# A two-layer decoder trunk in float32: a second seven-product slice in the feed-forward blocks, with its products set between plain ones

## The chip, the cores and the metric

The kernel runs on one core of one Trainium2 chip. The metric is the device time of one execution in microseconds (us); lower is better. TensorE (PE in the profile) multiplies, VectorE (DVE), ScalarE (ACT) and GpSimd (POOL) prepare its operands, SyncE (SP) issues most transfers from HBM.

## The reference

Two decoder layers on 256 tokens of width 2048, all in float32. `wide` below stands for 5632.

```
for l in range(2):
    h = rms_norm(x, attn_norm[l])
    za, zq, zk, zv, zc = split(h @ w_in[l])      # 2048 x 5632: gated mixer, attention, conv
    ya = gelu(za) -> u, v;  u * (tril(ws) @ layer_norm(v) + bs)      # 4 groups of 128
    yb = softmax(q0 k0) v - lam * softmax(q1 k1) v, with rotary q, k # 4 heads
    yc = bg * conv3(cg * hc)
    x = x + (group_rms(ya, yb, yc) * mix_norm[l]) @ w_out[l]         # 2048 x 2048
    h = rms_norm(x, ffn_norm[l])
    x = x + (silu(h @ w_gate[l]) * (h @ w_up[l])) @ w_down[l]        # 2048 x wide, wide x 2048
return rms_norm(x, final_norm)
```

## The kernel before

**Tiling.** Every weight matrix is cut into blocks of 512 x 512 (`CW = 512`): four weight tiles of 128 rows by 512 columns, 1 MB in float32, laid out so that a block is contiguous. The 256 tokens are two halves of 128 (`NT = 2`). TensorE holds a 128 x 128 piece of the activations and streams 512 weight columns through it.

**Splitting.** The matmuls take operands of type float32r. Each float32 operand is split into a high part of that type and the rest, the low part, and a product is three matmuls: high by high, low by high, high by low (`products`, L220 to L222). Weights are split on the fly, half a block (two weight tiles, 128 x 1024) at a time; this is a *job*: ScalarE writes the high part `wh` (L169), VectorE subtracts it for the low part `wl` (L170). A plain job feeds 2 token halves x 2 weight tiles x 3 = 12 matmuls. The pool `wsp` holds five split halves, and `ahead(4)` emits the split of the job four ahead before the matmuls of the present one: a split can begin when the job five before it has left its buffer.

**Seven products.** In each feed-forward block `f` (512 of the 5632 hidden columns, eleven blocks a layer) the gate and up weights of one of the four slices `k` of 512 input rows (`SEVEN = 1`, the second) are multiplied by Strassen's scheme. It takes the 2 x 2 blocks (two token halves by two halves of the slice's rows; gate and up as the columns) with seven products in place of eight. Each of the seven has one job of its own and 6 matmuls (`seven_products`). The sums of activation blocks (`block_sums`) are made once a layer; the sums of weight halves are made for each block: three by VectorE (L164), and one by a transfer that adds in flight (`accum_op=ALU.add`, on POOL's queue, L175). Four products go to the tiles `p` and are combined on VectorE (L828 to L831), three go straight into the accumulators `c`.

**Order.** Each engine works its own queue in order; a scheduler places the instructions of the program in these queues near to program order. Side work (norms, transposes, attention) is put into a list by `later`, and `step` runs one entry after each job. `need` runs the list as far as an operand requires. The input projection's column chunks are worked in the order of `IN_ORDER`: two value chunks, then query and key chunks of attention, chunk 1 (the gated mixer's `v`: gelu, layer norm), 9, 10 and 8 (conv), 0 (the gated mixer's `u`). What follows a chunk, such as the layer norm of chunk 1 (L724 to L753), is emitted when its matmuls are done.

**Loads.** One transfer of 1 MB per block on SP's queue (512 KB and 256 KB at the start), four buffers of 1 MB (`wfp`). After each feed-forward block the 16 pieces of its transposed result are moved by SP's queue as well (`moved_transposed`).

Of the kernel before, what the change touches and what calls it, by code (L numbers as in the profile page):

```python
# [18 lines left out]
P = 128  # L19
# [34 lines left out]
def trunk_kernel(ctx: ExitStack, tc, x, positions, w_in, gmlp_ln_g, gmlp_ln_b,  # L54
# [11 lines left out]
    wfp = ctx.enter_context(tc.tile_pool(name="wf", bufs=4))  # L66
    wsp = ctx.enter_context(tc.tile_pool(name="wsplit", bufs=5))
    bpool = ctx.enter_context(tc.tile_pool(name="blk", bufs=27))
# [11 lines left out]
    IN_ORDER = [6, 7, 2, 4, 3, 5, 1, 9, 10, 8, 0]  # L80
# [8 lines left out]
    SEVEN = 1  # L89
    wsrc = []  # L90
    onto = {}
    jobs = []

    def wblock(w, k, c):
        return w[c, k].rearrange("p (k c) -> p k c", k=4)

    def plain(src):
        jobs.extend((len(wsrc), h, None) for h in range(2))
        wsrc.append(src)

    def seven(src1, src2):

        i, j = len(wsrc), len(wsrc) + 1
        onto[len(jobs)] = (i, j)
        jobs.extend([(i, 0, None), (j, 0, (j, 1)), (j, 1, None), (i, 1, None), (i, 0, None),
                     (j, 1, (i, 0)), (i, 1, (j, 1))])
        wsrc.extend([src1, src2])

    for l in range(L):
        for n, k in PAIR if l else FIRST:
            plain(wblock(w_in[l], k, IN_ORDER[n]))
        for c in IN_ORDER[2:]:
            for k in range(NX):
                plain(wblock(w_in[l], k, c))
        for n, k in PAIR:
            plain(wblock(w_out[l], MIX_ORDER[k], n))
        for c in range(2, NX):
            for k in MIX_ORDER:  # L120
                plain(wblock(w_out[l], k, c))
        for hv in PARTS:
            for f in hv:
                for k in range(NX):
                    if k == SEVEN:
                        seven(wblock(w_gate[l], k, f), wblock(w_up[l], k, f))
                    else:
                        plain(wblock(w_gate[l], k, f))
                        plain(wblock(w_up[l], k, f))
            for c, k in pair(len(hv)):  # L130
                plain(wblock(w_down[l], hv[k], c))
            for c in range(2, NX):
                for f in hv:
                    plain(wblock(w_down[l], f, c))

    wfull, whalf, lows = {}, {}, {}
    state = {"load": 0, "split": 0, "use": 0}

    def load_weights(n):
        while state["load"] < min(n, len(wsrc)):  # L140
            i = state["load"]
            wf = wfp.tile([P, 4, CW], F32, tag="wf", name=f"wf{i}")
            w = 2 if i < 4 else 4
            for k in range(0, 4, w):
                nc.sync.dma_start(out=wf[:, k:k + w], in_=wsrc[i][:, k:k + w])
            wfull[i] = wf
            state["load"] += 1

    def load_weight_part(i, k0, k1, queue=nc.sync):
        if i not in wfull:  # L150
            wfull[i] = wfp.tile([P, 4, CW], F32, tag="wf", name=f"wf{i}")
            state["load"] = max(state["load"], i + 1)
        queue.dma_start(out=wfull[i][:, k0:k1], in_=wsrc[i][:, k0:k1])

    def split_weights(n):
        while state["split"] < min(n, len(jobs)):
            j = state["split"]
            i, h, more = jobs[j]
            load_weights(max(i, more[0] if more else 0) + 1)
            wf = wfull[i][:, 2 * h:2 * h + 2]  # L160
            if more is not None:
                i2, h2 = more
                with tc.issue_after(lows[j - 2].ins):
                    nc.vector.tensor_tensor(wf, wf, wfull[i2][:, 2 * h2:2 * h2 + 2], op=ALU.add)  # L164
# [8 lines left out]
            lows[j] = state["dve"]  # L173
            if j in onto:
                nc.gpsimd.dma_start(out=wf, in_=wsrc[onto[j][1]][:, 0:2], accum_op=ALU.add)  # L175
            state["split"] += 1

    def ahead(n):

        j = min(state["use"] + n, len(jobs) - 1)  # L180
        split_weights(j + 1)
        load_weights(jobs[state["use"]][0] + 4)
# [53 lines left out]
    def seven_products(dst, operand, sums):  # L236

        sh, sl = sums
        S = [[[x[:, n, k] for k in range(2)] for x in (sh, sl)] for n in range(4)]
        lhs = [block(operand, 0, 0), S[2], S[3], block(operand, 1, 0), S[0], S[1], block(operand, 1, 1)]  # L240
        for (acc, first, last), x in zip(dst, lhs):
            ahead(4)
            products(acc, *x, state["use"], first, last)
            whalf.pop(state["use"])
            state["use"] += 1
            step()
# [32 lines left out]
    load_weight_part(0, 0, 1, nc.scalar)  # L279
# [24 lines left out]
    for c in range(NX):  # L304
        xt = blk([P, 4, S], f"xt{c}")
        th, tl = blk([P, 4, S], f"tha0_{c}", F32R), blk([P, 4, S], f"tla0_{c}", F32R)
        for k in range(0, 4, 2):
            nc.sync.dma_start(out=xt[:, k:k + 2], in_=x_t[c, :, k:k + 2])
            if c == 0:
                if k == 0:  # L310
                    nc.sync.dma_start(out=gT, in_=gains)
                load_weight_part(0, 1 + k, 2 + k)
                if k == 0:
                    load_weight_part(0, 2, 3)
# [15 lines left out]
        load_weights(min(c + 1, 3))  # L330
# [6 lines left out]
    def rstd(dst, src, scale, eps, n):  # L337

        nc.gpsimd.tensor_scalar(dst, src, scale, eps, op0=ALU.mult, op1=ALU.add)
        nc.gpsimd.tensor_tensor(dst, dst, neghalf[:, :n], op=ALU.pow)  # L340

    def rotary_tables(pos_i, frq):
# [34 lines left out]
        turns(ang, 1.0)  # L377
        for j in range(4):
            axpy(ang, n, -cs[j], ang)
        V.tensor_tensor(ang, ang, rem, op=ALU.add)  # L380
        turns(ang, 1.0)
        for j in range(4):
            axpy(ang, n, -cs[j], ang)
        lim = 3.1415925
        V.tensor_scalar(ang, ang, lim, -lim, op0=ALU.min, op1=ALU.max)
# [9 lines left out]
        return waves  # L395
# [79 lines left out]
    def moved_transposed(src, dst, key, gap):  # L475
# [28 lines left out]
    def block_sums(stat, key, gcol):  # L504
# [16 lines left out]
        def split():  # L521
            nc.scalar.copy(sh, sr)
            nc.vector.tensor_tensor(sl, sr, sh.bitcast(F32), op=ALU.subtract)
            stat["sums"] = (sh, sl)
# [32 lines left out]
    def norm_chunk(c, ssq, gcol, stat, tag, sums=False):  # L557
# [3 lines left out]
        if sums:  # L561
            block_sums(stat, (tag, "sums"), gcol + 4 * c)(o)
# [26 lines left out]
    waves = rotary_tables(*tabs)  # L589

    for l in range(L):
# [21 lines left out]
        later(token_scales, ("r", l))  # L613
        lng, lnb, cw, wT = layer_loads(l)
        if l == 0:
            later(lambda: lambdas(load_lambda()))
        later(rotary_scales, ("rt", l), wait=17 if l == 0 else 0)
# [179 lines left out]
        def projected(c, acc):  # L797
            add_residual(acc, c)
            norm_chunk(c, ssq, 32 + 16 * l, stat, f"f{l}", c == SEVEN)

# [7 lines left out]
        for hi, hv in enumerate(PARTS):  # L808
            mids = {}
            for f in hv:  # L810
                P1, P5, P7, P6 = (trp.tile([P, CW], F32, tag="tr", name=f"p{n}_{f}") for n in (1, 5, 7, 6))
                C = [[accp.tile([P, CW], F32, tag="acc", name=f"c{f}_{n}{t}") for t in range(NT)] for n in range(2)]
                for k in range(SEVEN):
                    need(fkeys[k])
                    for n in range(2):
                        weight_tile(C[n], stat[fkeys[k]], [k == 0] * NT, False)
                need(fkeys[SEVEN])
                need((f"f{l}", "sums"))
                alone = (True, True)
                seven_products([(P1, *alone), (P7, *alone), (C[1][0], False, False), (C[0][0], False, False),  # L820
                                (P5, *alone), (P6, *alone), (C[0][1], False, False)],
                               stat[fkeys[SEVEN]], stat["sums"])
                if rf is None:
                    rf = token_rstd(ssq, "rf")
                sg, mid = blk([P, NT, CW], "sg"), blk([P, NT, CW], "mid")

                nc.scalar.copy(sg[:, 0], P1)
                nc.vector.tensor_tensor(mid[:, 0], sg[:, 0], P6, op=ALU.add)  # L828
                nc.vector.tensor_tensor(sg[:, 1], mid[:, 0], P7, op=ALU.add)
                nc.vector.tensor_tensor(mid[:, 0], P5, mid[:, 0], op=ALU.subtract)  # L830
                nc.vector.tensor_tensor(mid[:, 1], P5, sg[:, 1], op=ALU.subtract)  # L831
                rest = range(SEVEN + 1, NX)
                for k in rest:
                    need(fkeys[k])
                    for n in range(2):
                        weight_tile(C[n], stat[fkeys[k]], [False] * NT, k == rest[-1])
                        for t in range(NT if k == rest[-1] else 0):
                            if n == 0:
                                nc.vector.tensor_tensor(sg[:, t], sg[:, t], C[0][t], op=ALU.add)
                                nc.scalar.activation(sg[:, t], sg[:, t], AF.Silu, scale=rf[:, t:t + 1])  # L840
                            else:
                                nc.vector.tensor_tensor(mid[:, t], mid[:, t], C[1][t], op=ALU.add)
                for t in range(NT):
# [97 lines left out]
```

## Time and profile before

| | |
|---|---|
| median of 3 runs | 2123.53 us (2121.87 to 2125.17) |
| the profiled execution | 2121.89 us, of which the span from the first to the last instruction is 2119.8 us |
| TensorE | busy 2098.0 us, 99% of the span, 9264 matmuls |
| VectorE / ScalarE / GpSimd | 74% / 54% / 9% |
| mean granted TensorE clock | 0.997 of full speed |
| transfers | 440.54 MB, mean 208 GB/s |

The busy times of engines overlap, so they don't add up to the span. A matmul's busy time includes the end of its pipeline, which the next one covers; its true cost is the distance between the starts of two. A VectorE instruction likewise is listed a little longer than its slot when the next one follows at once.

### The profile page before, as it was taken

Reading aid. Unit: us, or ns where it says so; the run is one execution under the profiler, and the core shown is the slowest. Engines: PE = TensorE matmul, PEld = TensorE weight load, DVE = VectorE, ACT = ScalarE, POOL = GpSimd, SP = SyncE. Lnnn points to the kernel's source line nnn. Section 1 sums busy time; section 2 is a strip of 40 time slices with the busy share of each in tenths; the row PEclk is TensorE's granted clock in tenths of the full one; section 3 lists DMA queues with packets and bytes.
Section 4 is the critical chain, followed back from the end, with each engine's and each line's share of the span. In section 5 each row is a group of like instructions: output and inputs, shape, how many; then the busy total and the mean of one; then the engine's idle time right before and its main releaser. Section 6 shows DMA issues by size and latency. Waiting matters only on the chain.

```text
span 2119.8 us, 25036 instructions
## 1 busy us (share of the span) xinstructions
PE 2098.0 (99%) x9264; PEld 1735.2 (82%) x9264; DVE 1559.2 (74%) x1926; ACT 1137.6 (54%) x1479; POOL 201.0 (9%) x199
## 2 busy tenths in 40 slices
PE   8999999999999999999999999999999999999998
PEld 7887888888888888888888878888888888888886
DVE  5787778877567775678767878788775678756874
ACT  6556468555444543454755664675554454534453
POOL 6123410000000000000001234000000000000002
PEclk9999999999999999999999999999999999999999
DMA  8654555676556656566565445556655566655663
GB/s 317 240 177 161 179 211 176 219 250 218 199 180 245 220 203 221 205 222 204 204 235 190 160 158 197 201 186 247 219 200 220 207 220 215 227 204 208 212 231 123
DMA packets 83013, 440.54 MB, mean 208 GB/s; under 512 B 13518, under 2 KB 25294, under 8 KB 34252
## 3 DMA queue, kind: packets, MB, share of 16 engines
q1 hardware_dynamic: 79580, 427.16, 55.3%
q0 software_dynamic: 3168, 11.54, 3.2%
q8 instruction: 72, 1.18, 0.2%
q14 instruction: 49, 0.40, 0.1%
q10 hardware_dynamic: 144, 0.26, 0.0%
HBM read 423.19 MB, written 2.10 MB: 201 GB/s over the span
## 4 chain that ended last, share of the span: by engine, by line
PE 86%; POOL 2%; DVE 2%; ACT 1%; issue 1%; DMA 0%; SPq 0%; POOLq 0%; ACTq 0%
PE acc L221 14%; PE acc L220 14%; PE acc L222 14%; PE c L221 13%; PE c L220 13%; PE c L222 13%; PE p L221 2%; PE p L220 2%; PE p L222 2%; DVE wl L170 1%; PE op L679 0%; ACT wh L169 0%; DMA x<-xh 0%; ACT bom L456 0%; POOL gsq L573 0%
## 5 line engine op out<-in xcount | busy, mean ns | idle before, releaser
L170 DVE TENSOR_TENSOR wl<-wf,wh 128x1024 fp32r<-128x1024 f32 (+1 forms) x836 | 1029.5, 1245 | 455.7 <-ACT wh L169 451.6
L169 ACT CAST wh<-wf 128x1024 fp32r<-128x1024 f32 (+1 forms) x836 | 868.4, 1050 | 837.4 <-PE acc L222 397.9
L220 PE MATMUL c<-wh,thf 128*128 128x512 f32 x1144 | 445.0, 389 | 0.0
L221 PE MATMUL c<-wl,thf 128*128 128x512 f32 x1144 | 445.0, 389 | 0.0
L222 PE MATMUL c<-wh,tlf 128*128 128x512 f32 x1144 | 445.0, 389 | 0.0
L220 PE MATMUL acc<-wh,tha 128*128 128x512 f32 x704 | 280.6, 399 | 1.4 <-ACT wh L169 1.4
L221 PE MATMUL acc<-wl,tha 128*128 128x512 f32 x704 | 275.4, 391 | 2.9 <-DVE wl L170 2.9
L222 PE MATMUL acc<-wh,tla 128*128 128x512 f32 x704 | 275.3, 391 | 0.0
L220 PE MATMUL acc<-wh,thd 128*128 128x512 f32 x704 | 273.9, 389 | 0.0
L221 PE MATMUL acc<-wl,thd 128*128 128x512 f32 x704 | 273.9, 389 | 0.0
L222 PE MATMUL acc<-wh,tld 128*128 128x512 f32 x704 | 273.9, 389 | 0.0
L220 PEld LDWEIGHTS c<-wh,thf 128*128 128x128 f32 x1144 | 214.7, 188 | 44.6
L222 PEld LDWEIGHTS c<-wh,tlf 128*128 128x128 f32 x1144 | 214.8, 188 | 44.5
L221 PEld LDWEIGHTS c<-wl,thf 128*128 128x128 f32 x1144 | 214.8, 188 | 44.5
L221 PEld LDWEIGHTS acc<-wl,tha 128*128 128x128 f32 x704 | 133.0, 189 | 31.1 <-DVE wl L170 4.2
L220 PEld LDWEIGHTS acc<-wh,tha 128*128 128x128 f32 x704 | 132.7, 189 | 29.2 <-ACT wh L169 1.9
L222 PEld LDWEIGHTS acc<-wh,tla 128*128 128x128 f32 x704 | 132.7, 188 | 28.4
L220 PEld LDWEIGHTS acc<-wh,thd 128*128 128x128 f32 x704 | 132.2, 188 | 27.4
L222 PEld LDWEIGHTS acc<-wh,tld 128*128 128x128 f32 x704 | 132.2, 188 | 27.4
L221 PEld LDWEIGHTS acc<-wl,thd 128*128 128x128 f32 x704 | 132.2, 188 | 27.4
L175 POOL DMA_DIRECT2D wf<-in_w_up_dram x22 | 19.4, 880 | 1324.3 <-DVE wl L170 1324.3
L221 PE MATMUL acc<-wl,thm 128*128 128x512 f32 x256 | 99.7, 390 | 0.1
(193 smaller groups left out, 1867.9 us busy)
## 6 DMA issues: line engine op xcount, KB each, us to landing
wf<-in_w_gate_dram SPq DMA_DIRECT2D x88, 1024.0 KB, 4.8
wf<-in_w_up_dram SPq DMA_DIRECT2D x88, 1024.0 KB, 6.3
wf<-in_w_down_dram SPq DMA_DIRECT2D x88, 1024.0 KB, 4.9
wf<-in_w_in_dram SPq DMA_DIRECT2D x84, 1024.0 KB, 4.8
wf<-in_w_out_dram SPq DMA_DIRECT2D x32, 1024.0 KB, 4.7
wf<-in_w_up_dram POOLq DMA_DIRECT2D x22, 512.0 KB, 5.7
bod<-btd SPq DMA_DIRECT2D x352, 32.0 KB, 1.9
wf<-in_w_in_dram SPq DMA_DIRECT2D x6, 512.0 KB, 8.1
```

The costliest lines, as they stand in the source:

```text
L169: state["act"] = nc.scalar.copy(wh[:, k:k + w], wf[:, k:k + w])
L170: state["dve"] = nc.vector.tensor_tensor(wl[:, k:k + w], wf[:, k:k + w], wh[:, k:k + w].bitcast(F32), op=ALU.subtract)
L175: nc.gpsimd.dma_start(out=wf, in_=wsrc[onto[j][1]][:, 0:2], accum_op=ALU.add)
L220: nc.tensor.matmul(acc, xh[k], wh[:, k, :], start=first and k == 0, stop=False)
L221: nc.tensor.matmul(acc, xh[k], wl[:, k, :], start=False, stop=False)
L222: nc.tensor.matmul(acc, xl[k], wh[:, k, :], start=False, stop=last and k == 1)
```

## The change

- `SEVEN` becomes a list: block 0 of a layer keeps slice 1 alone, blocks 1 to 10 use the scheme for slices 0 and 1. Both slices add into the same four tiles `p`, which are combined once.
- The jobs of a block are written out by `ffn_order`: of the eight last plain jobs, the first seven are each followed by one product of each seven-product slice (order 1, 7, 5, 6, 3, 2, 4). Products are taken job by job (`half_products`).
- For slice 0 the sum for product 7 is made by a second transfer that adds in flight (`plus`); product 6 and product 4 have their sums from VectorE, as in slice 1, where product 7 has it too.
- Weights are loaded half a block (512 KB) at a time into tiles of the common pool `blk` (35 in place of 27 tiles of 4 KB a partition, `wfp` is gone), by a window of 20 half-job units and at most 10 tiles.
- Half of the 16 moves after a block go to POOL's queue.
- `IN_ORDER`: the gated mixer's chunk 1 and conv's chunk 9 change places.
- At the start, the second half of the rotary table's arithmetic (`near`) goes behind the first token scale on POOL.
- At the end, the last norm's sum over the first three chunks is taken ahead.

```diff
-    IN_ORDER = [6, 7, 2, 4, 3, 5, 1, 9, 10, 8, 0]
+    IN_ORDER = [6, 7, 2, 4, 3, 5, 9, 1, 10, 8, 0]
...
-    SEVEN = 1
+    WINDOW = 20
+    ROOM = 10
+    SEVEN = [[1], [0, 1]]
+    P1, P7, P5, P6, P3, P2, P4 = range(7)
+    def ffn_order():
...
+            own = [("plain", f, k, n, h) for k in range(NX) if k not in sv for n in range(2) for h in range(2)]
+            for j, it in enumerate(own):
+                items.append(it)
+                if 0 <= j - len(own) + 8 < 7:
+                    items.extend(("seven", f, j - len(own) + 8, k) for k in sv)
...
+        if p == P1:
+            onto[len(jobs)] = whalf_of(w_up[l], k, f, 0)
+            job(half(0, 0), size=1)
...
+        elif p == P7:
+            if k == 0:
+                i = half(1, 0)
+                plus[i] = whalf_of(w_up[l], k, f, 1)
+                first[i] = len(jobs) - 6
+                job(i, size=1)
+            else:
+                job(half(1, 0), half(1, 1), size=1)
...
+    def load_weights(upto, room=None):
+        while state["load"] < len(loads) and first[loads[state["load"]]] < upto and (
+                room is None or len(wfull) < room):
+            i = loads[state["load"]]
+            load_piece(i, 0, 2)
+            if i in plus:
+                nc.gpsimd.dma_start(out=wfull[i], in_=plus[i], accum_op=ALU.add)
...
-        load_weights(min(c + 1, 3))
+        load_weights(2 * min(c + 2, 4))
...
+        def near():
+            with tc.issue_after(state["r"].ins):
+                turns(ang, 1.0)
...
         def moves(a):
             for q in range(4):
-                nc.sync.dma_start(out=o[32 * q:32 * q + 32, a],
-                                  in_=b[32 * a:32 * a + 32, q].rearrange("p k t i -> p (k t i)"))
+                (nc.gpsimd, nc.sync)[q % 2].dma_start(out=o[32 * q:32 * q + 32, a],
+                                                      in_=b[32 * a:32 * a + 32, q].rearrange("p k t i -> p (k t i)"))
...
+            if p == P6:
...
+                nc.vector.tensor_tensor(mid[:, 0], sg[:, 0], p6, op=ALU.add)
+                nc.vector.tensor_tensor(sg[:, 1], mid[:, 0], p7, op=ALU.add)
+                nc.vector.tensor_tensor(mid[:, 0], p5, mid[:, 0], op=ALU.subtract)
+                nc.vector.tensor_tensor(mid[:, 1], p5, sg[:, 1], op=ALU.subtract)
...
-        nc.vector.tensor_reduce(r[:, 0:1], ssq[:, t], axis=AX.X, op=ALU.add)
-        rstd(r[:, 1:2], r[:, 0:1], 1.0 / D, RMS_EPS, 1)
+        nc.vector.tensor_scalar(r[:, 2:3], ssq[:, t, c:c + 1], 1.0 / D, r[:, 1:2], op0=ALU.mult, op1=ALU.add)
+        nc.gpsimd.tensor_tensor(r[:, 3:4], r[:, 2:3], neghalf[:, :1], op=ALU.pow)
```

**VectorE's queue in a steady feed-forward block.** Before, in block 4, from the last sum of weight halves to the transposes of the block's result (`wl` is the low part of a job, `p` and `c` are products and accumulators, `mid` and `sg` the halves of the gated result):

```order
L828 TENSOR_TENSOR mid<-sg,p_4_5001 128x512
L170 TENSOR_TENSOR wl_5143<-wf_5080,wh_5142 128x1024
L829 TENSOR_TENSOR sg<-mid,p_4_5000 128x512
L170 TENSOR_TENSOR wl_5160<-wf_5093,wh_5159 128x1024
L830 TENSOR_TENSOR mid<-p_4_4999,mid 128x512
L831 TENSOR_TENSOR mid<-p_4_4999,sg 128x512
```

```order
L842 TENSOR_TENSOR mid<-mid,c_10_5004 128x512
L842 TENSOR_TENSOR mid<-mid,c_11_5005 128x512
L844 SCALAR_TENSOR_TENSOR mid<-mid,rf,sg 128x512 x2
L485 STREAM_TRANSPOSE btd_4_5305<-mid 128x4x4x32 x2
L170 TENSOR_TENSOR wl_5318<-wf_5269,wh_5317 128x1024
```

With the change, VectorE's queue where block 4 ends and block 5 goes on (L224 is the sum of two weight halves; the first `wl` behind the transposes is product 7 of slice 0 of block 5, the sum and the `wl` behind it are product 7 of slice 1):

```order
L904 TENSOR_TENSOR mid_5279<-mid_5279,c4_10_5276 128x512
L904 TENSOR_TENSOR mid_5279<-mid_5279,c4_11_5277 128x512
L906 SCALAR_TENSOR_TENSOR mid_5279<-mid_5279,rf_3466,sg_5278 128x512 x2
L549 STREAM_TRANSPOSE btd_0_4_5603<-mid_5279 128x4x4x32 x2
L230 TENSOR_TENSOR wl263_5618<-wf236_5367,wh263_5617 128x1024
L224 TENSOR_TENSOR wf237_5494<-wf237_5494,wf238_5496 128x1024
L230 TENSOR_TENSOR wl264_5643<-wf237_5494,wh264_5642 128x1024
L230 TENSOR_TENSOR wl265_5663<-wf239_5515,wh265_5662 128x1024
L230 TENSOR_TENSOR wl266_5676<-wf233_5427,wh266_5675 128x1024
L230 TENSOR_TENSOR wl267_5694<-wf234_5439,wh267_5693 128x1024
L230 TENSOR_TENSOR wl268_5706<-wf240_5527,wh268_5705 128x1024
```

The end of a block used to be followed by the plain jobs of slice 0; now it stands two jobs ahead of a sum whose `wl` follows at once.

**VectorE's queue around the gated mixer's layer norm, layer 0.** Before (`bst`, `mv`, `vn` are the layer norm of chunk 1, `se` and `st` the softmax of attention's second pair of heads):

```order
L732 BN_STATS bst<-vg 128x6 x4
L734 BN_AGGR mv<-bst 128x2 x4
L170 TENSOR_TENSOR wl_1592<-wf_1505,wh_1591 128x1024
L737 TENSOR_SCALAR vn<-vg,mv,rs 128x128 x4
L170 TENSOR_TENSOR wl_1618<-wf_1505,wh_1617 128x1024
L732 BN_STATS bst<-vg 128x6 x4
L734 BN_AGGR mv<-bst 128x2 x4
L653 TENSOR_TENSOR se<-sp,mask 128x2x128
L737 TENSOR_SCALAR vn<-vg,mv,rs 128x128 x4
L654 TENSOR_REDUCE st<-se 128x2
```

With the change, the same place on VectorE (`oy` is attention's output, behind the softmax):

```order
L751 TENSOR_SCALAR oy<-op,sq 128x256
L798 BN_STATS bst<-vg 128x6 x4
L800 BN_AGGR mv<-bst 128x2 x4
L230 TENSOR_TENSOR wl_1892<-wf_1703,wh_1891 128x1024
L751 TENSOR_SCALAR oy<-op,sq 128x256
L803 TENSOR_SCALAR vn<-vg,mv,rs 128x128 x4
L798 BN_STATS bst<-vg 128x6 x4
L800 BN_AGGR mv<-bst 128x2 x4
L230 TENSOR_TENSOR wl_1923<-wf_1734,wh_1922 128x1024
L803 TENSOR_SCALAR vn<-vg,mv,rs 128x128 x4
L751 TENSOR_SCALAR oy<-op,sq 128x256
L230 TENSOR_TENSOR wl_1950<-wf_1765,wh_1949 128x1024
```

All softmax rows of that pair now stand ahead of the layer norm; behind it stand scalings of attention's output and further splits.

## Rows read from the trace of the kernel before

**Rows 1.** Head of the page: span, and busy time, share, instructions of two engines.

```profile
span 2119.8 us, 25036 instructions
...
PE 2098.0 (99%) x9264; PEld 1735.2 (82%) x9264; DVE 1559.2 (74%) x1926; ACT 1137.6 (54%) x1479; POOL 201.0 (9%) x199
```

**Rows 2.** Waits of all engines: in total, times, longest, us.

```profile
DVE wl L170 <- ACT wh L169: 451.6, 389, 2.6
ACT wh L169 <- PE acc L222: 397.9, 258, 2.6
...
DVE rq L608 <- POOL r L340: 9.2, 1, 9.2
...
DVE vn L737 <- POOL rs L340: 7.5, 4, 2.6
```

**Rows 3.** PE's instructions in block 0's plain jobs, first and last of 90.

```profile
399.81 0.39 PE L220 MATMUL c<-wh,thf 128*128 128x512 f32 x1
...
419.99 0.39 PE L222 MATMUL c<-wh,tlf 128*128 128x512 f32 x1
```

**Rows 4.** VectorE's instructions in block 4, start and duration in us.

```profile
505.13 0.68 DVE L828 TENSOR_TENSOR mid<-sg,p 128x512 f32<-128x512 f32 x1
505.73 1.22 DVE L170 TENSOR_TENSOR wl<-wf,wh 128x1024 fp32r<-128x1024 f32 x1
506.87 0.68 DVE L829 TENSOR_TENSOR sg<-mid,p 128x512 f32<-128x512 f32 x1
...
527.93 1.41 DVE L844 SCALAR_TENSOR_TENSOR mid<-mid,rf,sg 128x512 f32<-128x512 f32 x2
529.25 1.30 DVE L485 STREAM_TRANSPOSE btd<-mid 128x512 f32<-128x512 f32 x2
530.48 2.32 DVE L170 TENSOR_TENSOR wl<-wf,wh 128x1024 fp32r<-128x1024 f32 x2
```

**Rows 5.** Costliest groups by line: ScalarE's high part of a job.

```profile
L169 ACT CAST wh<-wf 128x1024 fp32r<-128x1024 f32 (+1 forms) x836 | 868.4, 1050 | 837.4 <-PE acc L222 397.9
```

**Rows 6.** DMA issues: count, KB each, median us from issue to landing.

```profile
wf<-in_w_gate_dram SPq DMA_DIRECT2D x88, 1024.0 KB, 4.8
...
wf<-in_w_up_dram POOLq DMA_DIRECT2D x22, 512.0 KB, 5.7
...
xs<-in_x_dram SPq DMA_DIRECT2D x4, 512.0 KB, 12.1
```

**Rows 7.** Two stretches: busy time, count by engine, then clock, DMA share, GB/s.

```profile
329.00:384.00 55.00, 55.00 (x245) 45.53 (x244) 49.59 (x71) 41.78 (x68) 1.98 (x3) 1.00 0.56 196
370.00:540.00 170.00, 170.00 (x752) 140.77 (x751) 136.66 (x143) 90.24 (x93) 2.65 (x3) 1.00 0.63 219
```

**Rows 8.** The pauses in layers 0 and 1: TensorE's first instruction behind each.

```profile
196.14 1.22 PE L679 MATMUL op<-v,aT 128*128 128x256 f32 x2 [3.77 <-DVE st L658]
...
1246.26 0.70 PE L679 MATMUL op<-v,aT 128*128 128x256 f32 x2 [4.11 <-DVE st L658]
```

**Rows 9.** Stretches behind the pauses, columns as in rows 7.

```profile
195.70:199.10 3.40, 2.96 (x8) 2.39 (x9) 3.03 (x6) 2.91 (x8) 0.66 (x1) 0.50 0.70 287
1247.00:1250.40 3.40, 3.40 (x10) 2.65 (x9) 2.67 (x4) 2.32 (x6) 1.68 (x2) 0.50 0.43 176
```

**Rows 10.** PE's instructions at the start that waited.

```profile
14.36 0.73 PE L220 MATMUL acc<-wh,tha 128*128 128x512 f32 x2 [1.13 <-ACT wh L169]
15.79 0.50 PE L221 MATMUL acc<-wl,tha 128*128 128x512 f32 x1 [0.70 <-DVE wl L170]
...
49.87 0.50 PE L221 MATMUL acc<-wl,tha 128*128 128x512 f32 x1 [1.37 <-DVE wl L170]
```

**Rows 11.** The end: the last token half's norm.

```profile
2113.27 0.19 POOL L339 TENSOR_SCALAR rl<-rl 128x1 f32<-128x1 f32 x1 [4.59 <-DVE rl L888]
2113.54 0.56 POOL L340 TENSOR_TENSOR rl<-rl,neghalf 128x1 f32<-128x1 f32 x1
2114.13 1.15 ACT L897 ACTIVATE xf<-xf,rl 128x1024 f32<-128x1024 f32 x1 [1.14 <-POOL rl L340]
```

More of the change, by code (lines that the diff above doesn't have):

```diff
@@ L90, in trunk_kernel, with whalf_of, source @@
+    FFN = ffn_order()
     wsrc = []
+    first = []
+    plus = {}
     onto = {}
     jobs = []
[L94 to L98, printed above, removed]
+    at = [0]
+    def whalf_of(w, k, c, h):
+        return w[c, k].rearrange("p (k c) -> p k c", k=4)[:, 2 * h:2 * h + 2]
+    def source(src):
         wsrc.append(src)
[L101 to L109, printed above, removed]
+        first.append(None)
+        return len(wsrc) - 1
@@ L122, in trunk_kernel @@
[L122 to L134, printed above, removed]
+                plain(w_out[l], k, c)
@@ new lines, in trunk_kernel @@
+        for it in FFN:
+            if it[0] == "plain":
+                _, f, k, n, h = it
+                job(source(whalf_of((w_gate, w_up)[n][l], k, f, h)))
+            elif it[0] == "seven":
+                seven(l, *it[1:])
+            else:
+                hv = PARTS[it[1]]
+                for c, k in pair(len(hv)):
+                    plain(w_down[l], hv[k], c)
+                for c in range(2, NX):
+                    for f in hv:
+                        plain(w_down[l], f, c)
@@ L136, in trunk_kernel @@
+    last = dict((i, j) for j, pair_ in enumerate(jobs) for i in pair_ if i is not None)
+    loads = sorted(range(len(wsrc)), key=lambda i: (first[i], i))
     wfull, whalf, lows = {}, {}, {}
     state = {"load": 0, "split": 0, "use": 0}
[L139 to L146, printed above, removed]
-            state["load"] += 1
@@ L234, in weight_tile, with half_products @@
             step()
[L236 to L246, printed above, removed]
+    def half_products(terms):
+        ahead(4)
+        for acc, x, starts, ends in terms:
+            products(acc, *x, state["use"], starts, ends)
+        whalf.pop(state["use"])
+        state["use"] += 1
+        step()
     def chunk(stat, keys, tail=0):
@@ L807, in trunk_kernel @@
         rf = None
[L808 to L822, printed above, removed]
+        now = {}
@@ L832, in trunk_kernel @@
[L832 to L842, printed above, removed]
@@ L875, in trunk_kernel @@
                     added(c, acc)
-        stat, ssq = stat2, ssq2
+            for key in dkeys:
+                mids.pop(key)
+            return (stat2, ssq2, acc, fin, xf) if lastpart else None
+        for it in FFN:
+            if it[0] == "plain":
+                if it[1] != now.get("f"):
+                    begin(it[1])
+                plain_half(*it[1:])
+            elif it[0] == "seven":
+                seven_half(*it[1:])
+            else:
+                ended = down(it[1])
+        stat, ssq, acc, fin, xf = ended
     flush()
```

201 lines of the change are left out of this document (143 added, 58 removed).

## The prediction, written before the changed kernel ran

> **What bounds the kernel now.** I read the page's head first: TensorE (PE) is busy 99% of the span, VectorE (DVE) 74% [rows 1]. Next the waits: DVE's large idle sum is spent on ScalarE's (ACT's) high parts, and ACT's on PE giving a buffer back [rows 2]. So the preparing engines run ahead and are held by the five buffers; PE sets the pace. The reader should then get the true price of a matmul from the instruction list: 90 in a row start within 20.18 us, (419.99 - 399.81)/89 = 0.2267 us each, not the 0.39 listed [rows 3]. A plain job is 12 x 0.2267 = 2.72 us, a seven-product job 1.36 us. Last, the places where PE did wait: a pause in each layer's attention [rows 8], the start [rows 10] and the tail behind the last matmul [rows 11].
>
> **Matmuls removed.** Blocks 1 to 10 of both layers, 20 blocks, trade eight products of slice 0 for seven: 6 matmuls fewer each, 120 in all. As long as PE stays the pace-maker this is 120 x 0.2267 = 27.2 us.
>
> **Does DVE keep up?** This is the step on which most rests. DVE slots, from start to start in block 4 [rows 4]: a half-size operation 505.73 - 505.13 = 0.60; a job's low part 506.87 - 505.73 = 1.14, and a sum of weight halves has its size; the multiply with two inputs and a scalar (529.25 - 527.93)/2 = 0.66; a transpose (530.48 - 529.25)/2 = 0.615.
> - A block before: PE 12 plain and 7 short jobs, 186 x 0.2267 = 42.17 us. DVE 19 low parts, 3 sums and the low part of the block before's result, 23 x 1.14 = 26.22; 8 half-size 4.80; 1.32; 1.23; together 33.6 us, 80%, which agrees with 136.66 of 170 us [rows 7].
> - A block after: PE 8 plain and 14 short jobs, 180 x 0.2267 = 40.81 us. DVE 22 low parts, 5 sums and the same rest: 28 x 1.14 = 31.92, plus 7.35, together 39.3 us, 96%.
>
> The margin of 1.5 us is then cut by one forced wait. Where a sum is followed directly by its own low part, DVE idles while ACT makes the high part, about 1.05 us [rows 5]. The other sums come in pairs, so the second covers the high part of the first; product 7 of slice 1 stands alone, right behind a block's end. The chain there, from the end of a block's last matmul: 2 x 0.60, 1.32, 1.23, a low part 1.14, the sum 1.14, ACT 1.05, the low part 1.14 = 8.2 us; PE needs it after the next block's first five jobs (plain, short, short, plain, short): 2 x 2.72 + 3 x 1.36 = 9.5 us. It holds by 1.3 us, less semaphore delays. DVE's period is 39.3 + 1.05 = 40.3 against PE's 40.8. I take PE as the bound, at no cost. Bounds: nothing, or, if DVE loses another 2 us a block to waits that I can't see, 20 x (42.3 - 40.8) = 30 us. Since the five buffers let DVE lag by some microseconds within a block, a local excess is absorbed; only the period counts.
>
> ACT was busy 53% in these stretches (90.24 of 170) [rows 7]; three more casts of 1.05 a block fit. POOL is busy 9% [rows 1]; per block it gains two adding transfers and eight moves, and has 40 us. In the output projection DVE and ACT also make slice 0's activation sums: on DVE four quarter-size operations under 0.60 and one of 1.14, below 3.6 us, where DVE had 55 - 49.6 = 5.4 us free [rows 7]. I take nothing; if that cover is gone, up to 3 us in each layer.
>
> **Loads.** Half-size transfers double SP's issues. Per block 16 loads and 3 adding transfers of 512 KB, 10.0 MB in 40.8 us, 244 GB/s; before, 8.9 MB in 42.2 us. The engines were 63% busy at 219 GB/s [rows 7], so about 70% now. An adding transfer landed 5.7 us after issue [rows 6]. Product 1 of slice 1 is split some 1.4 us ahead of the block's start, so its sum with the up half is there at about 5 us; DVE comes to it (product 5) at about 12 us. That wait is hidden with 5 us or more to spare, and I cost loads at nothing.
>
> The Trainium skill speaks against half-size loads: "DMA: Bandwidth & Descriptors", section "Measured (HBM→SBUF, 128 partitions, SWDGE, issued from GpSimd)", says to batch transfers to 1 MiB or more for at least 75% of peak. Its fit under "Anatomy of one DMA" (about 2.0 us plus bytes over 436 GB/s) would make an estimated 3.2 us per 512 KB, 61 us for 19 in a row. The trace shows 219 GB/s from transfers that overlap, so I don't take them in a row.
>
> **The pauses in attention.** Before, the gated mixer's layer norm sits in DVE's queue ahead of the softmax of attention's second head pair, and waits there for POOL (the row of `vn`) [rows 2]. PE stands 3.77 and 4.11 us [rows 8], and behind each pause the granted clock is 0.50, the level of 1.2 GHz, for 3.4 us, in which PE was busy 2.96 and 3.40 us [rows 9]; at 2.4 GHz half of that would do, so 1.48 + 1.70 are lost. Together 11.1 us. With chunk 9 first, whose follow-up is two ACT copies, the softmax stands ahead of the layer norm, as the order shows. What is late next are splits behind the layer norm; DVE can lag there by about four plain jobs less ACT's and DVE's own 2.4, so some 8 us, and its waits for POOL were at most 2.6 us each [rows 2]. I take the whole 11.1. Bounds: 11.1 and, if a pause appears elsewhere, 0.
>
> **Start and end.** PE's wait of 1.37 us at 49.87 us [rows 10] comes from DVE standing 9.2 us at the first token scale behind the rotary tables on POOL [rows 2]; `near` moves behind it: -1.4. The second weight block is loaded ahead of the second input slice, which shortens the 1.13 + 0.70 us at 14 us [rows 10]; but `xs` loads now stand early in SP's queue between weights (12.1 us to landing [rows 6]) and ACT reads them in order ahead of casts. I take 0 for the pair, from -1.8 to +3. At the end the first POOL step goes, 2113.54 - 2113.27 = 0.27, and ACT's last scaling is half as long, 1.15 to about 0.7 [rows 11]: -0.7.
>
> **Sum.** Profiled execution 2121.9 - 27.2 - 11.1 - 1.4 - 0.7 = 2081.5. The median of the runs lies 1.6 above that execution, so 2083.
>
> **Rivals.**
> - *DVE binds in the two-slice blocks.* For: 96% by slots, in an in-order queue with waits on ACT and PE. Against: the chain above closes by 1.3 us. With 1 to 2 us of further idle a block its period is 41.3 to 42.3: 10 to 30 us of the gain are gone, 2093 to 2113, middle about 2098.
> - *The pause only moves.* The layer norm still waits for POOL, which then also serves attention's scales; if PE again stands about 4 us in each layer, 11 us come back: 2094.
> - *Slower: the adding transfers come late.* Three share POOL's queue with the moves and the fabric with more loads. DVE waits for them in order, so each microsecond beyond some 12 us to landing lengthens DVE's period. Attention, start and end give back 13 us, so slower than before needs a block of 42.17 + 13/20 = 42.8 us, 2.5 us above DVE's 40.3: a landing near 14 us in place of 5.7. Even the crowded start showed 12.1 [rows 6]. At 15 us: block about 43.5, 2121.9 + 20 x 1.33 - 13.2 + 1.6 = 2137.
> - *Half-size loads halve the transfer rate.* The DMA engines would need twice 70% of a block, 57 us, 16 us more than PE: 20 x 16 = 320 us, about 2400. Nothing in the rows suggests it. The rule of the Trainium skill cited above ("DMA: Bandwidth & Descriptors", section "Measured (HBM→SBUF, 128 partitions, SWDGE, issued from GpSimd)") points this way.
>
> **How the numbers follow.** The forecast (PE keeps the pace, pauses gone) 0.60, with a range of its own of 2077 to 2090 from the start's bounds and small waits; DVE binds 0.20; the pause moves 0.13; late transfers 0.05; slow loads 0.02. From 2076 to 2107 holds the first, the third and about three fifths of the second. Within 0.2% (4 us) is what a measurement here can't tell from no change. Faster by more than that: the first three cases, 0.92; slower: most of the last two, 0.05; the rest, 0.03, the same.
>
> **What would show it.** Right: 120 matmuls fewer, PE gaps near 0.227 us through blocks 1 to 10, DVE near 95% there, no PE wait above 2 us in either attention stage and a granted clock of 1.00 there. Wrong: PE waiting for `wl` or `wh` in the blocks; DVE waiting for `wf` of an adding transfer; ACT's casts waiting for loads; a PE wait on `op`, `ap` or `wl` behind chunk 1.

## The result, and the profile after

The changed kernel takes 2092.22 us (median of four runs, 2090.70 to 2092.50), the kernel before 2123.86 (four runs beside it, 2121.87 to 2125.17): a ratio of 0.985 with a 95% interval of 0.9833 to 0.9867, so 31.6 us faster. The forecast was 2083, in a range of 2076 to 2107: the direction and the main term hold, and 9 us of the gain are missing.

The head of the page after: span, then busy time, share and instructions of each engine, the packets, MB and share of 16 engines' time of two DMA queues (q0 carries POOL's transfers), and some DMA issues (count, KB, median us to landing). It answers to [rows 1, 6].

```profile
span 2090.5 us, 26504 instructions
...
PE 2070.7 (99%) x9144; PEld 1709.2 (82%) x9144; DVE 1675.0 (80%) x2042; ACT 1194.8 (57%) x1545; POOL 323.5 (15%) x413
...
q1 hardware_dynamic: 125852, 421.40, 56.2%
q0 software_dynamic: 14560, 38.29, 9.7%
...
wf<-in_w_gate_dram SPq DMA_DIRECT2D x176, 512.0 KB, 7.3
...
wf<-in_w_up_dram POOLq DMA_DIRECT2D x62, 512.0 KB, 8.2
...
bod<-btd POOLq DMA_DIRECT2D x176, 32.0 KB, 2.9
```

PE has 120 matmuls fewer, as said. To see where the time went, I cut both spans at the first and the last matmul into `p` or `c` of each layer (the down projections between the runs of blocks lie within the rows of the blocks):

| stage | before, us | after, us | difference |
|---|---|---|---|
| start, mixing of layer 0 | 358.33 | 354.84 | -3.5 |
| feed-forward blocks, layer 0 | 637.61 | 624.01 | -13.6 |
| last down projection, mixing of layer 1 | 412.22 | 408.92 | -3.3 |
| feed-forward blocks, layer 1 | 637.61 | 624.01 | -13.6 |
| last down projection, to the last matmul's start | 65.28 | 65.49 | +0.2 |
| from there to the end of the span | 8.77 | 13.24 | +4.5 |

The feed-forward blocks give 2 x 13.6 = 27.2 us, to a tenth what 120 x 0.2267 promised. The mixing stages give 6.8 where 12.5 was forecast (pauses and start), and the end loses 4.5 where 0.7 was to be won.

Three stretches of the changed kernel, one two-slice block each, columns as in [rows 7]:

```profile
397.00:437.80 40.80, 40.80 (x182) 33.78 (x180) 39.19 (x41) 24.80 (x26) 7.09 (x12) 1.00 0.78 253
437.80:478.60 40.80, 40.80 (x182) 33.78 (x180) 39.44 (x41) 25.02 (x27) 6.62 (x12) 1.00 0.81 257
478.60:519.40 40.80, 40.80 (x182) 33.78 (x180) 39.45 (x41) 25.02 (x27) 4.03 (x9) 1.00 0.71 232
```

PE (second figure) is busy for all of each 40.8 us, VectorE (fourth) for 39.2 to 39.5: the prediction's slots gave 39.3. The forced wait is there too. VectorE's instructions at a block's end (the last column names the idle time before one):

```profile
440.85 1.30 DVE L549 STREAM_TRANSPOSE btd<-mid 128x512 f32<-128x512 f32 x2
442.07 1.18 DVE L230 TENSOR_TENSOR wl<-wf,wh 128x1024 fp32r<-128x1024 f32 x1
443.17 1.21 DVE L224 TENSOR_TENSOR wf<-wf,wf 128x1024 f32<-128x1024 f32 x1
445.58 2.36 DVE L230 TENSOR_TENSOR wl<-wf,wh 128x1024 fp32r<-128x1024 f32 x2 [1.20 <-ACT wh L229]
```

1.20 us idle where 1.05 was forecast. PE has no wait at all in the feed-forward blocks of either layer.

The waits of PE in the mixing of layer 0 (100 to 330 us) and of layer 1 (1140 to 1380 us), one row for each:

```profile
PE acc L286 <- DVE wl L230: 1.1, 3, 0.6
...
PE acc L286 <- DVE wl L230: 1.3, 3, 0.6
```

Both pauses of [rows 8] are gone, and with them the half clock of [rows 9]: the granted clock is 1.00 in both stages. In their place stand three small waits a layer for the low part `wl`, near the last chunk of the input projection and the first jobs of the output projection.

And the end. Instructions of the program's last line by engine (duration in ns as least, median, most; then first and last start), of the changed kernel:

```profile
L1054 POOLq DRAIN  x3: 46/102/10232, 2079.5 to 2090.2; - x3
L1054 SPq DRAIN  x3: 7/7/7, 2085.3 to 2090.0; - x3
```

and of the kernel before:

```profile
L937 POOLq DRAIN  x3: 40/102/2484, 2113.5 to 2119.6; - x3
L937 SPq DRAIN  x3: 7/7/7, 2119.0 to 2119.3; - x3
```

Each engine closes with a DRAIN, and all wait for the last of them. SP reaches its own when the output has landed. Before, POOL's long DRAIN (2.48 us from 2113.5) was over by then. Now it lasts 10.23 us from 2079.5, to 2089.7, while SP was ready at 2085.3: the 4.4 us between are idle on every engine. The chain of waits doesn't show it: its last piece is VectorE's at 2080.87.

### The profile page after: what moved, and what is told of

Its sections match the earlier page's. It is cut to its first block, busy times and chain, and to the rows that moved or that the text cites. A ratio compares the mean times of both kernels' runs of the same rounds, so it can differ in the third digit from the quotient of the medians.

```text
span 2090.5 us, 26504 instructions
## 1 busy us (share of the span) xinstructions
PE 2070.7 (99%) x9144; PEld 1709.2 (82%) x9144; DVE 1675.0 (80%) x2042; ACT 1194.8 (57%) x1545; POOL 323.5 (15%) x413
## 3 DMA queue, kind: packets, MB, share of 16 engines
q1 hardware_dynamic: 125852, 421.40, 56.2%
## 5 line engine op out<-in xcount | busy, mean ns | idle before, releaser
L230 DVE TENSOR_TENSOR wl<-wf,wh 128x1024 fp32r<-128x1024 f32 (+1 forms) x896 | 1093.3, 1245 | 332.6 <-ACT wh L229 316.0
L229 ACT CAST wh<-wf 128x1024 fp32r<-128x1024 f32 (+1 forms) x896 | 926.1, 1050 | 751.4 <-PE acc L287 403.7
L285 PE MATMUL c<-wh,thf 128*128 128x512 f32 x904 | 351.7, 389 | 0.0
L286 PE MATMUL c<-wl,thf 128*128 128x512 f32 x904 | 351.7, 389 | 0.0
L287 PE MATMUL c<-wh,tlf 128*128 128x512 f32 x904 | 351.7, 389 | 0.0
L287 PEld LDWEIGHTS c<-wh,tlf 128*128 128x128 f32 x904 | 169.7, 188 | 35.3
L285 PEld LDWEIGHTS c<-wh,thf 128*128 128x128 f32 x904 | 169.7, 188 | 35.2
L286 PEld LDWEIGHTS c<-wl,thf 128*128 128x128 f32 x904 | 169.7, 188 | 35.2
L286 PEld LDWEIGHTS acc<-wl,tha 128*128 128x128 f32 x704 | 132.3, 188 | 34.1 <-DVE wl L230 7.5
L554 POOL DMA_DIRECT2D bod<-btd x176 | 87.4, 508 | 298.9 <-DVE btd L549 146.5
L224 DVE TENSOR_TENSOR wf<-wf,wf 128x1024 f32<-128x1024 f32 x106 | 126.0, 1216 | 0.1
```

The lines of the kernel that those rows point to most:

```text
L224: nc.vector.tensor_tensor(wf, wf, wfull[more], op=ALU.add)
L229: state["act"] = nc.scalar.copy(wh[:, k:k + w], wf[:, k:k + w])
L230: state["dve"] = nc.vector.tensor_tensor(wl[:, k:k + w], wf[:, k:k + w], wh[:, k:k + w].bitcast(F32), op=ALU.subtract)
L285: nc.tensor.matmul(acc, xh[k], wh[:, k, :], start=first and k == 0, stop=False)
L286: nc.tensor.matmul(acc, xh[k], wl[:, k, :], start=False, stop=False)
L287: nc.tensor.matmul(acc, xl[k], wh[:, k, :], start=False, stop=last and k == 1)
```

## The experiments

Gains below are differences of medians to the kernel before, run on the same chip beside each; the changed kernel's is 31.6 us.

**Moves between the queues.** What lengthens POOL's DRAIN? With the change POOL issues 62 adding transfers and 176 moves; before, 22 transfers.

```diff
-                (nc.gpsimd, nc.sync)[q % 2].dma_start(out=o[32 * q:32 * q + 32, a],
+                nc.sync.dma_start(out=o[32 * q:32 * q + 32, a],
```

> The changed kernel with all 16 moves of a block's result back on SP's queue, so POOL issues 62 transfers in place of 238. Theory A: POOL's closing DRAIN lasts longer the more transfers POOL has issued (22 before: 2.48 us, 238 after: 10.23 us, so about 0.036 us each): here about 3.9 us, which ends before SP's last wait, the time from the last matmul's start to the end of the span falls from 13.2 to about 8.8 us, and the kernel takes about 2087.8 us. Theory B: the long DRAIN comes from the new code of the last norm, not from the transfers: it stays near 10 us and the time near 2092.2. Theory C: the moves delay the loads behind them on SP's in-order queue: PE waits in the blocks, over 2092.2.

Measured: 2097.6 us, a gain of 25.5. The DRAIN fell to 3.58 us, and the last matmul stands 8.79 us ahead of the end. But PE now waits in the blocks and longest in the last down projection; its instructions there:

```profile
2040.58 0.50 PE L285 MATMUL acc<-wh,thd 128*128 128x512 f32 x1 [2.86 <-ACT thd L560]
2042.03 0.79 PE L287 MATMUL acc<-wh,tld 128*128 128x512 f32 x1 [0.60 <-DVE tld L561]
```

SP's queue just before:

```profile
2005.61 0.33 SPq L205 DMA_DIRECT2D wf<-in_w_down_dram  x1
2020.91 5.76 SPq L554 DMA_DIRECT2D bod<-btd  x8
2026.76 0.53 SPq L205 DMA_DIRECT2D wf<-in_w_down_dram  x1
2027.33 4.94 SPq L554 DMA_DIRECT2D bod<-btd  x8
2032.68 10.82 SPq L205 DMA_DIRECT2D wf<-in_w_down_dram  x13
```

SP stands from 2005.9 to 2020.9 at moves whose data isn't ready, and spends 11 us on issuing 16 of them, with 14 loads behind. ACT then waited 3.9 us for a `w_down` half that had not landed, and PE for ACT. So theories A and C both hold: the DRAIN is short, and the queue pays for it with some 12 us of PE's time (by the distances between the starts of its matmuls, from 400 us on); 3.0 of them are lost at the half clock that follows the wait shown.

All 16 on POOL's queue is the same edit with `nc.gpsimd`:

> The changed kernel with all 16 moves on POOL's queue: POOL issues 414 transfers in place of 238. Theory A (the closing DRAIN grows by 0.036 us a transfer): DRAIN about 16.5 us, the end 6.3 us later, about 2098.5 us. Theory B (not the transfers): DRAIN near 10 us, time near 2092.2.

Measured: 2090.4 us, a gain of 32.7, and a DRAIN of 4.84 us: more transfers, but a shorter DRAIN. Theory A in its linear form falls, and theory B with it. The end is 4.4 us shorter than in the changed kernel, but the time only 1 to 2 us: in the profile the blocks take 1.2 and 0.8 us more and the mixing of layer 1 1.3 us more, at small waits for `wl`. One move in four on SP, on top of the spread copies told of below:

```diff
-                nc.gpsimd.dma_start(out=o[32 * q:32 * q + 32, a],
+                (nc.gpsimd, nc.sync)[q == 3].dma_start(out=o[32 * q:32 * q + 32, a],
```

> The kernel with all moves on POOL and spread copies (2087.6 us), but one move in four on SP's queue: POOL issues 326 transfers. POOL's closing DRAIN took 2.48, 3.58, 6.97, 10.23 and 4.84 us behind 22, 62, 198, 238 and 414 transfers, the same to 0.01 us in every kernel with the same count. If it grows up to some count and starts anew behind it, 326 lies in between: either over 10.23 (no new start yet, end at least 13.2 us behind the last matmul, 2092 us or more) or under 4.84 (started anew, end 8.8 us, 2088). If the mean over the moves on SP delays loads as in the run with all moves on SP, PE waits of 1 us or so in some blocks come on top.

Measured: 2088.73 us, a gain of 34.1; the DRAIN took 7.54 us, in neither of the two ranges, and PE has no waits in the blocks. And the moves alone, in the kernel before:

```diff
-                nc.sync.dma_start(out=o[32 * q:32 * q + 32, a],
+                (nc.gpsimd, nc.sync)[q % 2].dma_start(out=o[32 * q:32 * q + 32, a],
```

> The kernel before with half of the 16 moves of each block on POOL's queue and nothing else changed: POOL issues 198 transfers, as in the changed kernel with one slice, whose closing DRAIN took 6.97 us. If the number of transfers alone sets the DRAIN: 6.97 us here, starting with the last POOL step some 6.3 us ahead of the end, so the end comes some 1.4 us later, about 2124.5. If the new code of the last norm matters: DRAIN near 2.5 us and 2123. If moves on SP's queue delayed loads in the kernel before as they do in the changed one: faster, by some microseconds.

Measured: 2123.32 us beside 2122.46, a ratio of 1.0006 (0.9996 to 1.0016); its DRAIN:

```profile
L937 POOLq DRAIN  x3: 46/102/6969, 2113.2 to 2120.7; - x3
```

6.97 us, as in the changed kernel with one slice, which has the same transfers and the new last norm. So the DRAIN goes by what POOL has issued, not by the code at the end. Taking half of the moves off SP's queue gained nothing here, since the blocks take 637.61 us a layer either way: the third expectation falls. All counts together:

| adding transfers + moves on POOL | DRAIN, us | last matmul to end, us |
|---|---|---|
| 22 + 0 (before) | 2.48 | 8.77 |
| 62 + 0 | 3.58 | 8.79 |
| 22 + 176 (two kernels) | 6.97 | 9.98, 10.20 |
| 62 + 176 (four kernels) | 10.23 | 13.24 |
| 62 + 264 | 7.54 | 10.54 |
| 62 + 352 (five kernels) | 4.84 | 8.80 to 9.02 |

Of the counts tried, 238 transfers give the longest; from there to 326 and to 414 it falls by 0.031 us for each one. Kernels with the same transfers on POOL have the same length; by which rule it follows from them is open. It costs nothing as long as it ends before SP's last wait, some 8 us behind the last matmul's start.

**The order of chunks.** Undone in the changed kernel:

```diff
-    IN_ORDER = [6, 7, 2, 4, 3, 5, 9, 1, 10, 8, 0]
+    IN_ORDER = [6, 7, 2, 4, 3, 5, 1, 9, 10, 8, 0]
```

> The changed kernel with the input projection's chunks in the order of before (chunk 1 ahead of 9). By the prediction's price for the two pauses (their idle time and the half clock behind them, 11.1 us, nothing given back): 2103 us. By the comparison of the two traces, in which the two attention stages together gained only 6.2 us because about 2.3 us a layer came back as new waits of PE for the low part wl: about 2098.5 us, with pauses of about 4 us at the softmax and without the waits of 0.4 to 0.7 us near chunk 0. If the order is worth nothing: 2092.

Measured: 2098.4 us, a gain of 24.7: the order is worth 6.2 us by medians, 6.9 by gains. The pauses come back, as the waits of PE over the whole run show:

```profile
PE op L745 <- DVE st L724: 7.7, 2, 3.8
PE acc L286 <- DVE wl L230: 1.9, 4, 0.5
```

and behind the first of them the half clock (columns as in [rows 7]):

```profile
195.00:200.50 5.50, 5.50 (x14) 4.34 (x15) 3.75 (x6) 3.17 (x6) 1.69 (x2) 0.50 0.75 252
```

One chunk further, on top of all moves on POOL and spread copies:

```diff
-    IN_ORDER = [6, 7, 2, 4, 3, 5, 9, 1, 10, 8, 0]
+    IN_ORDER = [6, 7, 2, 4, 3, 5, 9, 10, 1, 8, 0]
```

> The kernel with all moves on POOL and spread copies, with chunk 10 ahead of chunk 1 as well (9, 10, 1, 8, 0), so that the layer norm of the gated mixer comes one chunk later and the first product of the conv one chunk earlier. Theory: PE's small waits for wl near the end of the input projection (0.6, 0.3 and 0.7 us a layer) come from DVE's work for chunks 8 and 0 alone, which doesn't move: same time, 2087.6. Rival: the layer norm's lag reaches as far as chunk 0; one chunk later makes it worse, by 1 to 3 us a layer: 2090 to 2094.

Measured: 2099.96 us, a gain of 22.9, 12 us worse than its base. Neither theory named the cause. The waits of PE:

```profile
PE mxp L814 <- POOL vn L807: 13.2, 2, 6.6
PE acc L286 <- DVE wl L230: 1.1, 3, 0.5
```

The three small waits a layer went (the 1.1 us left lie at the start), but PE stood 6.6 us a layer at the gated mixer's own matmuls, for the last step of the layer norm on POOL. POOL's instructions of it in layer 0:

```profile
224.84 1.08 POOL L400 TENSOR_SCALAR rs<-mv 128x4 f32<-128x4 f32 x1 [9.19 <-DVE mv L800]
...
234.47 5.58 POOL L806 TENSOR_TENSOR vn<-vn,lc 128x512 f32<-128x512 f32 x1 [1.23 <-DVE vn L803]
240.13 1.26 POOL L807 TENSOR_TENSOR vn<-vn,lc 128x512 f32<-128x512 f32 x1
```

The layer norm itself came one chunk later: POOL's first step of it starts at 224.84 us, in the changed kernel at 197.26. The conv's work didn't hold it up: POOL stood idle 9.19 us before that step. So the place of chunk 1 has a pause on either side: one chunk earlier PE waits for the softmax behind it, one later for the layer norm itself.

What makes the three small waits? ACT's instructions in the changed kernel, where the output projection begins:

```profile
272.05 1.05 ACT L229 CAST wh<-wf 128x1024 fp32r<-128x1024 f32 x1 [0.17 <-PE acc L287]
281.18 3.32 ACT L520 COPY bom<-btm 32x256 f32<-32x256 f32 x8 [8.08 <-DVE btm L512]
284.53 1.05 ACT L229 CAST wh<-wf 128x1024 fp32r<-128x1024 f32 x1
```

ACT stands 8.08 us at copies of a result that VectorE transposes only at 280; the casts are queued behind. First try, on top of all moves on POOL:

```diff
-                block_transposed(mx, M, (f"m{l}", 0), 64 + 16 * l, per=4, wait=1)
+                block_transposed(mx, M, (f"m{l}", 0), 64 + 16 * l, per=2, wait=1)
```

> The changed kernel with all 16 moves on POOL's queue and the gated mixer's transposed copies in two steps with a job between them in place of one step of eight copies on each of ACT and DVE. Theory: PE's wait of 0.7 us behind the first jobs of the output projection comes from ACT standing 3.3 us in those copies ahead of a cast; it goes in both layers, 1.5 us less than all moves on POOL, about 2089 us. Rival: the wait only moves to the next job: 2090.4.

Measured: 2087.56 us, a gain of 34.9. The time moved by 2 us, but not for the reason given: ACT's eight copies still stand in one row, the wait at the output projection is still 0.57 us, and the profiled run with all moves on POOL had had some other small waits that this one lacks. So the theory falls; nor did the wait move on to the next job, as the rival had it, and what the 2 us are isn't shown. Second try, on top of that:

```diff
-                block_transposed(yconv, M, (f"m{l}", 3), 64 + 16 * l + 12, per=2, wait=2)
+                block_transposed(yconv, M, (f"m{l}", 3), 64 + 16 * l + 12, per=2, wait=4)
...
-                block_transposed(mx, M, (f"m{l}", 0), 64 + 16 * l, per=2, wait=1)
+                block_transposed(mx, M, (f"m{l}", 0), 64 + 16 * l, per=2, wait=4)
```

> The kernel with all moves on POOL and spread copies, with the transposes of the conv's and of the gated mixer's result entered 2 and 3 jobs later in the list of side work, so that one more cast of ACT stands ahead of the copies that wait for them. In the trace of all moves on POOL with spread copies ACT stood 8.07 and 8.40 us at such copies for DVE's transposes, with the casts queued behind, and PE then waited 0.6, 0.3 and 0.7 us a layer for wl. Theory: these waits go, 1.6 us a layer with what is behind them, so some 3 us less than 2087.6: 2084.5. Rival: the lag is DVE's own work, and the waits stay or move: 2087.6.

Measured: 2084.09 us (2083.76 to 2086.75), a ratio to before of 0.9825 (0.9811 to 0.9838), a gain of 37.9. Of PE's six small waits one is left; the mixing of layer 0:

```profile
PE acc L286 <- DVE wl L230: 0.2, 1, 0.2
```

The theory priced the waits at 1.6 us a layer with what is behind them; by the starts of PE's matmuls 1.7 us came back in each of the two mixing stages, against the changed kernel. So the waits were ACT's place in its own queue, and no lack of VectorE's time. This is the fastest version, 6 us ahead of the changed kernel by gains.

**How near is VectorE to setting the pace?** One slice in all blocks, everything else as changed:

```diff
-    SEVEN = [[1], [0, 1]]
+    SEVEN = [[1], [1]]
```

> The changed kernel with one seven-product slice in every block (slice 1), all else as changed: 120 matmuls more, 20 adding transfers and 40 sums of weight halves fewer. If PE keeps the pace with two slices: 120 x 0.2267 = 27.2 us slower than the changed kernel, less about 0.7 us at the end for 20 transfers fewer on POOL: about 2118.7. If DVE already holds PE back with two slices by up to 0.5 us a block, 10 us of that are missing: about 2109.

Measured: 2114.49 us, a gain of 8.6. Each layer's feed-forward blocks take 637.61 us again, 13.60 more: 27.2 in all, so PE alone sets the pace with two slices. The end is 3.3 us shorter and the stretch up to layer 0's first block 1.7 us, so 22 us are left, as measured.

Extra work for VectorE in each two-slice block, six reductions as shown, or two with `p < 2`:

```diff
+    spare = cpool.tile([P, 1], F32, name="spare")
...
             if k != sv[-1]:
                 return
+            if f > 0 and p < 6:
+                with tc.issue_after(state["dve"].ins):
+                    nc.vector.tensor_reduce(spare, xs[:, 0, :CW], axis=AX.X, op=ALU.add)
```

> The changed kernel with two extra reductions of 128x512 on VectorE in each two-slice block (some 0.6 us each from start to start; their result isn't used). DVE was busy 39.4 of 40.8 us a block in the changed kernel and waited 1.2 us a block for ACT, so 40.6 of 40.8. Theory A (DVE is within 0.2 us a block of setting the pace, and the five buffers and the down projections between the runs of 3, 4 and 3 blocks let it make up some 6 us of lag): 41.8 us a block, a lag of 3 to 4 us by the end of a run, absorbed: 2092 to 2096 us. Without absorption: 20 x 1.0 more, about 2112. Theory B (DVE has slack that its busy time doesn't show): 2092.

> As the run before with six such reductions, 3.6 us a block. Theory A: DVE needs 44.2 us a block, 3.4 over PE; runs of 3, 4 and 3 blocks lose 10.2, 13.6 and 10.2 us, less some 6 us each that the buffers absorb: 16 us a layer, about 2125 us (2110 to 2160). Theory B (hidden slack): under 2097.

Measured: 2095.67 us with two (4.8 us of gain lost) and 2140.45 with six (49.6 lost, a ratio to before of 1.0083). The feed-forward blocks of the two layers take 626.8 and 626.4 us with two, 648.3 and 646.4 with six, where the changed kernel takes 624.0. PE's largest waits with six:

```profile
PE c L286 <- DVE wl L230: 18.8, 16, 1.2
PE c L285 <- ACT wh L229: 8.3, 24, 0.5
```

Theory A holds: of the 34 us a layer by which six reductions overload VectorE, 24 and 22 come out as time, and the buffers absorb 10 and 12. There was no hidden slack. The changed kernel stands where 1.2 us more on VectorE a block begins to show.

**The start.** The second half of the rotary tables back in its place, on top of all moves on POOL and spread copies:

```diff
-            with tc.issue_after(state["r"].ins):
-                turns(ang, 1.0)
+            turns(ang, 1.0)
...
-        return near, waves
+        near()
+        return None, waves
...
-        if l == 0:
-            later(near)
```

> The kernel with all moves on POOL and spread copies, with the second half of the rotary tables back at its place ahead of the first token scale. By the prediction's price: PE's wait of 1.4 us near 48 us comes back, 2089.0. By the trace of the changed kernel, where PE's waits in the first 60 us sum to as much as before (5.4 against 5.3 us over the pitch): the same, 2087.6.

Measured: 2088.4 us, a gain of 34.4. It decides nothing: in the order that came out the token scale still stood ahead of `near` in POOL's queue (at 29.9 us), so the edit undid nothing. It serves as a repeat of its base (2087.56). VectorE waits 1.5 us for that scale in both kernels, where it waited 9.2 before [rows 2]; so that moving `near` is what took this wait away is not shown.

## Why the prediction was right, and where it was not

The time lies in the stated range of 2076 to 2107, but above the 2077 to 2090 of the forecast's own case: its mechanism came out, but the terms for the pauses and the end are wrong. Below, "by the starts" means that a matmul's start is compared with the start of the same matmul in the other kernel.

- **Matmuls removed, -27.2:** right, in the trace and by undoing it.
- **VectorE keeps up, at no cost:** right, with the busy time (39.3) and the forced wait (1.05 against 1.20) both near. The rival that VectorE binds was false, but by little, as the extra reductions show.
- **Loads, nothing:** right. PE has no wait in the blocks, and VectorE none there for an adding transfer, which landed 8.2 us after issue, against the 14 us that the rival of late transfers needed. The rival of half-size loads at half the rate was false: with one slice and 512 KB loads the engines were 65% busy at 225 GB/s, before 63% at 219 [rows 7]. So the rule of the Trainium skill that spoke against them ("DMA: Bandwidth & Descriptors", section "Measured (HBM→SBUF, 128 partitions, SWDGE, issued from GpSimd)", figures for transfers that GpSimd issues) doesn't show here, where SP issues the loads: bytes for each busy microsecond of the engines are the same at either size. With two slices the blocks ran at 71 to 81%, where I had forecast 70%; I hadn't counted adding transfers as dearer than loads, and they are: with all moves on SP, so with nothing but adding transfers on q0, that queue took 8.5% of the engines' time for 32.5 MB; in the changed kernel q1 took 56.2% for 421.4 MB, half as much for a MB.
- **Pauses, -11.1: mis-sized, -6.7.** What the pauses cost was priced rightly. By the starts, layer 0 gains 3.9 us at the pause and 1.5 at the half clock behind it, layer 1 4.3 and 1.7, together 11.4. But the step "What is late next are splits behind the layer norm", which I costed at nothing, failed: 2.0 us came back in layer 0 and 2.6 in layer 1, of which 1.8 and 2.4 at the three small waits (1.1 and 1.3 us of idle time). They are the "PE wait on `op`, `ap` or `wl` behind chunk 1" that I had named as a sign of being wrong. Undoing the order cost 6.2 to 6.9 us, as much as was left. Nor was the lag where I had looked for it, behind the layer norm on VectorE: it is ACT standing at copies, with casts behind them; two later entries in the list of side work took all but 0.2 us of the idle time away.
- **Start, -1.4: -0.1 in this profile.** By the starts, the wait at 49.87 gave 1.6 us, and the two near 14 us [rows 10] 2.4. All of that was lost again between 19 and 36 us, the largest piece at a wait of 1.49 us for `wl`, ahead of which VectorE stands for the first token scale, still late, if less so than before:

```profile
32.18 0.21 DVE L672 TENSOR_SCALAR rq<-r 128x1 f32<-128x1 f32 x2 [1.54 <-POOL r L401]
...
33.65 0.50 PE L286 MATMUL acc<-wl,tha 128*128 128x512 f32 x1 [1.49 <-DVE wl L230]
```

ACT also reads `xs` ahead of casts there, the loss that the bound of +3 stood for; no run separates the two. Over the twelve profiles with the changed start, the 401st matmul starts at 93.86 to 95.98 us, on average at 94.91, and before at 96.02: some 1 us is gained on average.
- **End, -0.7: wrong in sign, +4.5.** Two errors. The step "ACT's last scaling is half as long" forgot that VectorE now makes two scalings in a row, from 2080.12 to 2081.27: 1.15 us, as long as ACT's one before [rows 11]. What the new norm saves up to the last output issue is 0.2 us, and where the DRAIN is hidden the end is as long as before (8.8 us). And I costed eight moves a block on POOL by POOL's time alone; what they leave behind in the closing DRAIN, 4.4 us, appeared in no term.

Of the rivals, "the pause only moves" was the nearest: two fifths of its cost did. The profiled executions differ by 29.3 us: -27.2 - 6.7 - 0.1, and 4.7 at the end, of which 0.2 ahead of the last matmul.

## What to carry over

Removing matmuls from a PE-bound stretch pays to the tenth of a microsecond, as long as the summed slots of the next engine stay below PE's period; a sum of slots from a few rows told that to 0.2 us. When a pause is removed, look through every in-order queue for the next instruction that stands and waits with casts or loads behind it (ACT's copies, SP's moves): here the cover lay in the queue's order, not in the engine's free time. And before adding many small transfers to POOL's queue, look at what its closing DRAIN takes and whether the end hides it.

## What the hardware did that I had not expected

POOL's closing DRAIN took 2.48 to 10.23 us, to 0.01 us the same in each kernel with the same transfers on POOL, longest at 238 transfers and shorter again at 326 and 414. The half clock behind a pause cost unlike amounts for like pauses. By the starts, against a kernel without the pause, the 3.77 and 4.11 us of before were followed by 1.5 and 1.7 us lost; with the order undone the two pauses of 3.83 and 3.82 us were followed by 2.7 us in layer 0 and 1.5 in layer 1. It came behind shorter waits too. With all moves on SP, 2.86 us and then 0.60 us of waiting were followed by 3.0 us lost; with six reductions the clock once fell behind waits of 0.29 and 1.20 us, 1.7 us apart, though not behind the thirteen other waits of 1.20 or 1.21 us in that run (columns as in [rows 7]; first all moves on SP, then six reductions):

```profile
2040.58:2048.00 7.42, 6.82 (x16) 5.00 (x17) 1.62 (x3) 1.04 (x1) 0.00 (x0) 0.54 1.03 417
...
517.00:521.60 4.60, 3.20 (x13) 2.06 (x12) 4.60 (x7) 2.64 (x3) 0.00 (x0) 1.00 0.62 213
521.69:525.00 3.31, 3.31 (x10) 2.65 (x11) 3.31 (x4) 3.31 (x5) 0.00 (x0) 0.68 0.04 11
```

In the changed kernel the granted clock stayed at 1.00 behind its longest wait, the 1.49 us at 33.65.
